# Cross attention scores and values, and the row sums of the prompt heads, as products of split parts

## The chip, the cores and the metric

The kernel runs on one core of a Trainium2 chip. The metric is device time in microseconds (us) of one execution; lower is better. The core has a matrix engine (TensorE, PE in the profile, with its weight loads listed as PEld), three engines for elementwise work (VectorE or DVE, ScalarE or ACT, GpSimd or POOL) and SyncE (SP), which issues most of the transfers. Each engine works through its own list of instructions in order, and semaphores tie the lists together.

## The reference, cut to what matters

One step of a decoder layer, for a prompt of 512 tokens and eight samples of four tokens that share all weights:

- h = RMSNorm(x); z = h W_in. Eight attention heads of 64 columns (three dilated patterns with a linear distance penalty) and four HGRN2 heads of 128. Each attention head's output is divided by its root mean square and multiplied by a gain.
- x = x + [attention ; HGRN2] W_out.
- Cross attention with four heads of 128 over a memory of 256 rows: cq = RMSNorm(x) W_cq; s = cq k^T / sqrt(128); p = softmax(s); x = x + (p v) W_co. For the prompt k and v are computed from `mem_prompt`; each sample has its own cached k and v.
- x = x + W_down( silu(conv3(RMSNorm(x) W_gate)) * (RMSNorm(x) W_up) ), then a last RMSNorm.

Everything is float32. The core of the cross attention is

```
cq = (c @ w_cq).reshape(B, T, X_H, X_DH)
s = jnp.einsum('bthd,bmhd->bhtm', cq, mem_k.astype(cq.dtype)).astype(f32) * (X_DH ** -0.5)
pr = jax.nn.softmax(s, axis=-1)
co = jnp.einsum('bhtm,bmhd->bthd', pr.astype(x.dtype), mem_v.astype(x.dtype)).reshape(B, T, X_W)
x = x + co @ w_co
```

and each attention head's norm is `a32 * rsqrt(mean(a32 * a32, -1) + EPS)` over its 64 columns.

## The kernel before, in words

**Layout.** Activations are held transposed: features on the 128 partitions, the 544 tokens (512 of the prompt, 32 of the samples) along the free dimension. Token columns are taken in two cuts, `CUTS` = 0 to 256 and 256 to 544.

**Split products.** The dense products do not use single precision operands. Each operand is split into a high part (a copy rounded to float32r, on ACT, or on DVE now and then) and a low part (the rest, a subtraction on DVE), and a product becomes three: high x high, high x low, low x high (`passes`, L922). Other products take their float32 operands directly, in one instruction of the program: scores, values, transposes' companions in the HGRN2 heads, sums over partitions.

**Stages.** First the input projections with the attention heads and the HGRN2 heads woven between them (tiles `ps_hv`, `ps_q`, `psS`, `psO` and so on), then memory keys and values (`ps_ck`, `ps_cv`), the output projection `ps_wo`, the cross attention (`ps_cq`, `ps_cp`, `ps_cpo`), its output projection `ps_co`, and the feed-forward part to the end.

**Order of the work.** The program is first recorded on a tape (`Tape`, L276) and then ordered: `due` (L417) gives each step a time by when it should begin, `order` (L462) goes through all engines with estimated durations, and `run` (L441) repeats this six times and keeps the best order. Dense products are marked main and keep the order in which they are written; all other PE work ("side" work: scores, transposes, values, row sums) is put between them when its inputs are estimated to be ready. So a change of any duration or of any operation can move every later step. Working tiles come from one pool of 71 buffers of 128 x 544 (`A`, L736, and `R`, L739, which gives a float32r tile of that pool); a step whose tile doesn't fit waits (`fits`, L544, `leaves_room`, L548). Scores, transposes and values write to a pool of five banks of PSUM (`PX`).

**The start** is kept in the order as written (L1036). SP loads the input blocks, the vectors, and the constants `cs`: identity, a matrix of ones, and `blk64`, ones in two diagonal blocks of 64, each 128 x 128. ACT squares each input block, DVE adds the squares, and `psr_mix` on PE sums them over partitions with the matrix of ones.

**Row sums.** `rsqrt_rows` (L964) multiplies squares with the ones or with `blk64`, so that every partition gets the sum, and ACT makes exp(-0.5 ln(.)) of it. `prompt_attention` (L1335) calls it for each of its four pairs of heads: `att` is the heads' output, `asq` its square, `psr_att` the sum, `ar` the factor.

**Cross attention.** `dense_by_half` (L942) computes the queries of all four heads for the first cut of the tokens, then of all four for the second; after each cut `cq_after` (L1911) runs for each head and calls `cross_prompt` (L1877), which handles 256 tokens: scores `ps_cp` (two products of 128 x 256), softmax into `cp`, four transposes `ps_cpt`, a copy `cpt`, values `ps_cpo` (two products of 128 x 256), and `split_psum` (L1809), which writes the high and low parts `coh` and `col` that the projection `ps_co` reads. The sample tokens have a path of their own: their queries go to `cqbd`, scores `ps_cs`, values `ps_cso`, gathered in `ps_cos`. `mk` and `mvt` are the prompt's memory keys and values.

Of the kernel before, what the change touches and what calls it, by code (L numbers as in the profile page):

```python
# [10 lines left out]
F32 = mybir.dt.float32  # L11
F32R = mybir.dt.float32r
AF = mybir.ActivationFunctionType
ALU = mybir.AluOpType
# [3 lines left out]
SEQ = 512  # L18
# [6 lines left out]
NMEM = 256  # L25
# [4 lines left out]
XH = 4  # L30
# [28 lines left out]
FW = N  # L59
# [663 lines left out]
def tile_decoder_step(ctx: ExitStack, tc: tile.TileContext, xT, memT, kwT, vw, s0, conv_in, mkT, mv, vecs, cst,  # L723
                      w_first, w_in, w_out, w_cq, w_ck, w_cv, w_co, w_gate, w_up, w_down,
                      yT, kT_out, vT_out, st_out, conv_out, mkT_out, mv_out, ss_out):
    nc = tape = Tape(tc.nc)

    one = ctx.enter_context(tc.tile_pool(name="one", bufs=1))
# [7 lines left out]
    def A(name, shape=None, dt=F32):  # L736
        return tape.tile(act, shape or [128, FW], dt, tag="a", name=name, bufs=NA)

    def R(name):  # L739
        return tape.tile(act, [128, FW], F32R, tag="a", name=name, bufs=NA)[:, :N]  # L740
# [24 lines left out]
    vec = tape.tile(one, [128, NVEC], F32, name="vec")  # L765
    nc.scalar.dma_start(vec[:, :KT], vecs[:, :KT])
    mid = CST_COLS["dbias"][0]
    cs = tape.tile(one, [128, mid], F32, name="cs")
    cs2 = tape.tile(strm, [128, NHELD - mid], F32, name="cs2")
    eps = tape.tile(one, [128, 1], F32, name="eps")  # L770
    nc.gpsimd.memset(eps, EPS)
# [3 lines left out]

    def C(name):
        lo, hi = CST_COLS[name]
        return cs[:, lo:hi] if hi <= mid else cs2[:, lo - mid:hi - mid]


    specs = []
# [171 lines left out]
    def split_into(hl, src, g, c0, c1):  # L953
        hi, lo = (t[:, c0:c1] for t in hl)
        nc.scalar.activation(hi, src, AF.Copy, scale=g)
        nc.vector.scalar_tensor_tensor(lo, src, g, hi.bitcast(F32), op0=ALU.mult, op1=ALU.subtract)

    def split_plain(src, name):
# [2 lines left out]
        nc.vector.tensor_tensor(lo, src, hi.bitcast(F32), op=ALU.subtract)  # L961
        return hi, lo

    def rsqrt_rows(acc, c0, c1, mat, width, r, name, rest=None):  # L964

        for n0, m in ((c0, c1 - c0),) if c1 - c0 <= 512 else CUTS:
            ps = (PX if rest is None else PDEC)(f"psr_{name}_{n0}")
            nc.tensor.matmul(ps[:, :m], mat, acc[:, n0:n0 + m], start=True, stop=rest is None)
            if rest is not None:
                nc.tensor.matmul(ps[:, :m], mat, rest[:, n0:n0 + m], start=False, stop=True)  # L970
            nc.scalar.activation(r[:, n0:n0 + m], ps[:, :m], AF.Ln, bias=eps, scale=1.0 / width)
            nc.scalar.activation(r[:, n0:n0 + m], r[:, n0:n0 + m], AF.Exp, scale=-0.5)

    class SumSq:
        def __init__(self, name, adder=nc.vector):
# [22 lines left out]
    def x_load(i, c0, c1):  # L998
        nc.sync.dma_start(xin[i][:, c0:c1], xT[128 * i:128 * i + 128, c0:c1])
# [4 lines left out]
    def warm_up(count, n=128):  # L1004

        for _ in range(count):
            nc.tensor.matmul(banks[0][1][:, :n], zero[:, :128], zero[:, :n], start=True, stop=True)
# [3 lines left out]
    def square(i):  # L1011
        if i:
            sqs.append(A(f"sq_mix{i}"))
        nc.scalar.activation(sqs[i][:, :N], xin[i][:, :N], AF.Square)

    def add_square(i):
        nc.vector.tensor_tensor(mix_acc[:, :N], mix_acc[:, :N], sqs[i][:, :N], op=ALU.add)
# [18 lines left out]
    with tape.as_written():  # L1036
        nc.scalar.preload_act_table_set(LN_SET)
        x_load(0, 0, 256)
        for c0, c1 in ((0, 128), (128, 384)):
            nc.sync.dma_start(wf[0][:, c0:c1], w_first[0][:, c0:c1])  # L1040
        x_load(0, 256, N)
        for i in range(1, KT):
            x_load(i, 0, N)
            nc.sync.dma_start(wf[i], w_first[i])
        nc.sync.dma_start(vec[:, KT:], vecs[:, KT:])
        nc.sync.dma_start(cs, cst[:, :mid])
        for i in range(3):
            ws.load(i)
        nc.sync.dma_start(cs2, cst[:, mid:NHELD])
        for _ in range(AHEAD - 1):  # L1050
            stream.load()
        zero = A("zero")
        nc.vector.memset(zero[:, :128], 0.0)
        with tape.main():
            warm_up(WARM)
        for i in range(KT):
            hi, lo = A(f"wfh{i}", [128, 384], F32R), A(f"wfl{i}", [128, 384], F32R)
            if i == 0:

                nc.vector.tensor_copy(hi[:, :128], wf[0][:, :128])  # L1060
                split_into(xs[0], xin[0][:, :256], V("norm_mix", 0), 0, 256)
                nc.scalar.copy(hi[:, 128:], wf[0][:, 128:])
                for c0, c1 in ((0, 128), (128, 384)):
                    nc.vector.tensor_tensor(lo[:, c0:c1], wf[0][:, c0:c1], hi[:, c0:c1].bitcast(F32), op=ALU.subtract)
                split_into(xs[0], xin[0][:, 256:N], V("norm_mix", 0), 256, N)
            else:
                split_into(xs[i], xin[i][:, :N], V("norm_mix", i), 0, N)
                nc.scalar.copy(hi, wf[i])
                nc.vector.tensor_tensor(lo, wf[i], hi.bitcast(F32), op=ALU.subtract)
            wf_hl.append((hi, lo))  # L1070
            if i > 1:
                square(i - 2)
            if i > 3:
                add_square(i - 3)
        square(KT - 2)
        add_square(KT - 3)
        square(KT - 1)
        add_square(KT - 2)
        add_square(KT - 1)

        for k in range(KT - 1):
            with tape.main():
                first_products(k)
        for n0, n in CUTS:
            ps = PD(f"psr_mix_{n0}")
            with tape.main():
                nc.tensor.matmul(ps[:, :n], C("ones"), mix_acc[:, n0:n0 + n], start=True, stop=True)
            nc.scalar.activation(r_mix[:, n0:n0 + n], ps[:, :n], AF.Ln, bias=eps, scale=1.0 / D)
            nc.scalar.activation(r_mix[:, n0:n0 + n], r_mix[:, n0:n0 + n], AF.Exp, scale=-0.5)
        with tape.main():  # L1090
            first_products(KT - 1)
# [243 lines left out]
    def prompt_attention(p, q, k, v):  # L1335
        pst = by_token(v, f"v{p}")
# [82 lines left out]
        po = PX(f"psO{p}")  # L1419
# [13 lines left out]
        att, sq, r = A(f"att{p}"), A(f"asq{p}"), A(f"ar{p}")  # L1433
        nc.scalar.copy(att[:, :SEQ], po)
        nc.scalar.activation(sq[:, :SEQ], po, AF.Square)
        rsqrt_rows(sq, 0, SEQ, C("blk64"), 64, r, f"att{p}")
        nc.vector.tensor_tensor(att[:, :SEQ], att[:, :SEQ], r[:, :SEQ], op=ALU.mult)
        att_parts(p)
        split_into(mixed[p], att[:, :SEQ], V("att_out_norm", p), 0, SEQ)
# [274 lines left out]
    ps = PX("psr_mem")  # L1714
# [7 lines left out]
    mk = [A(f"mk{i}", [128, 2, NMEM]) for i in range(2)]  # L1722
    mvt = [A(f"mvt{t}") for t in range(2)]
# [10 lines left out]
    for c in range(4):  # L1734
        ws.take()
        for i in range(2):
            hi, lo = (t.rearrange("p k c -> p (k c)") for t in ws.whole[ws.i - 1][i][:2])
            xh, xl = mems[2 * c + i]
            with tape.main():
                for t in range(2):  # L1740
                    tok = slice(128 * t, 128 * t + 128)
                    for j, (a, b) in enumerate(((xh, hi), (xl, hi), (xh, lo))):
                        nc.tensor.matmul(pcv[t], a[:, tok], b, start=(c == 0 and i == 0 and j == 0),
                                         stop=(c == 3 and i == 1 and j == 2))
# [60 lines left out]
    cqbd = tape.tile(strm, [128, NB, 4, 32], F32, tag="qbd", name="qbd_mem", bufs=1)  # L1805
    nc.gpsimd.memset(cqbd, 0.0)
    co_hl = [(R(f"coh{h}"), R(f"col{h}")) for h in range(XH)]

    def split_psum(h, ps, c0, c1):  # L1809
        hi, lo = (t[:, c0:c1] for t in co_hl[h])  # L1810
# [66 lines left out]
    def cross_prompt(h, part):  # L1877

        ps = PX(f"ps_cp{h}{part}")
        for a in range(2):  # L1880
            qb = 2 * part + a
            nc.tensor.matmul(ps[:, 256 * a:256 * a + 256], cqT[h][:, 128 * qb:128 * qb + 128],
                             mk[h // 2][:, h % 2, :], start=True, stop=True)
        if part:
            cross_sample_scores(h)
        pt = A(f"cp{h}{part}")
        den = softmax_exp(ps, pt, f"{h}{part}")
        softmax_scale(pt, den)
        pst = PX(f"ps_cpt{h}{part}")
        for c in range(2):  # L1890
            for a in range(2):
                nc.tensor.transpose(pst[:, 256 * c + 128 * a:256 * c + 128 * a + 128],
                                    pt[:, 256 * a + 128 * c:256 * a + 128 * c + 128], C("ident"))
        ptt = A(f"cpt{h}{part}")
        if part:
            nc.vector.tensor_copy(ptt[:, :512], pst)
        else:
            nc.scalar.copy(ptt[:, :512], pst)
        po = PX(f"ps_cpo{h}{part}")
        for c in range(2):  # L1900
            nc.tensor.matmul(po[:, :256], mvt[c][:, 128 * h:128 * h + 128], ptt[:, 256 * c:256 * c + 256],
                             start=c == 0, stop=c == 1)
        split_psum(h, po[:, :256], 256 * part, 256 * part + 256)

    cqT = [A(f"cq{h}") for h in range(XH)]

    def cq_evac(h, ps, n0, n):
        nc.vector.scalar_tensor_tensor(cqT[h][:, n0:n0 + n], ps[:, :n], 128.0 ** -0.5, r_cross[:, n0:n0 + n],
                                       op0=ALU.mult, op1=ALU.mult)

    def cq_after(h, c):  # L1911
        if c:
            nc.gpsimd.tensor_copy(cqbd[:, :, h, 4 * h:4 * h + 4],
                                  cqT[h][:, SEQ:N].rearrange("p (b t) -> p b t", t=TS))
        cross_prompt(h, c)
# [763 lines left out]
    for m in range(2 * LAST_PAIRS, KT):  # L2679
        held[m] = []  # L2680
        for c in range(0, k, 4):
            e = min(k - c, 4)
            t, hi, lo = (A(f"{n}z{m}_{c}", [128, e, 128], dt) for n, dt in (("wd", F32), ("wdh", F32R), ("wdl", F32R)))
# [21 lines left out]
    rest = [(m, c) for c in range(1, 2) for m in range(2 * LAST_PAIRS, KT)]  # L2705
    before.step(3)
    before.step(4)
    while rest:
        m, c = rest.pop(0)
# [81 lines left out]
```

## Time and profile before

| | |
|---|---|
| median of 3 runs | 807.85 us (807.83 to 808.33) |
| the profiled execution | 808.49 us, of which the span is 806.7 us |
| PE busy | 793.3 us, 98% of the span |
| DVE busy | 664.9 us, 82% |
| ACT busy | 466.8 us, 58% |
| POOL busy | 200.2 us, 25% |

The span is the time from the first to the last instruction that the profile records. Rows of the profile are read like this: "L718 PE MATMUL ps_cp<-mk,cq" is a matmul that writes tile ps_cp from mk and cq; L718 is the line of the recorder through which every operation passes, so tiles, not lines, tell operations apart. Matmuls overlap in the pipeline, so the mean of one record is longer than the time by which it moves the next; the rows of the chain, which give a start and a length for a whole run of matmuls, tell that.

### The profile page before, as it was taken

To read this page: it belongs to the slowest core of one execution; us is meant where nothing else is said; L and a number is where in the kernel's file an instruction comes from. 1 tells how busy PE (TensorE), PEld (TensorE's weight loads), DVE (VectorE), ACT (ScalarE), POOL (GpSimd) and SP (SyncE) were. 2 spreads that over 40 slices of the span, in tenths; PEclk is the share of its full clock that TensorE was granted. 3 is DMA by queue.
4 is the path that set the end of the run, shared out by engine and by line. 5 is a ranking of instruction groups with operands and counts; after the bars stand their busy time and mean duration, and the time that the engine had idled before them with its cause. 6 is when DMAs were issued, how large, how long until landed. Compare 5 with 4: busy or idle time off the path is not lost.

```text
span 806.7 us, 19149 instructions
## 1 busy us (share of the span) xinstructions
PE 793.3 (98%) x7432; PEld 745.7 (92%) x7432; DVE 664.9 (82%) x1484; ACT 466.8 (58%) x996; POOL 200.2 (25%) x282
## 2 busy tenths in 40 slices
PE   9999999999999999999999999999999999999995
PEld 8998878887888989999889999999999999999995
DVE  6899787488788885664579989998998998989973
ACT  7734468626458445544266657665665766668642
POOL 1131100031110200232134134442353352242023
PEclk9999999999999999999999999999999999999999
DMA  8744894998942355461654177778878878777203
GB/s 308 252 145 137 272 324 146 303 347 275 293 136 79 108 162 201 131 176 49 195 157 132 35 169 184 169 167 199 200 164 192 196 165 199 184 200 173 70 2 111
DMA packets 106699, 143.35 MB, mean 178 GB/s; under 512 B 7280, under 2 KB 73712, under 8 KB 106608
## 3 DMA queue, kind: packets, MB, share of 16 engines
q1 hardware_dynamic: 91296, 123.77, 48.4%
q0 software_dynamic: 14592, 17.83, 14.1%
q8 instruction: 58, 0.95, 0.5%
q10 hardware_dynamic: 720, 0.53, 0.2%
q14 instruction: 33, 0.27, 0.1%
HBM read 134.04 MB, written 8.07 MB: 176 GB/s over the span
## 4 chain that ended last, share of the span: by engine, by line
PE 89%; DVE 4%; ACT 3%; DMA 1%; issue 1%; SPq 0%; DVEq 0%; ACTq 0%
PE ps_au L718 7%; PE ps_ag L718 7%; PE ps_wo L718 6%; PE ps_aw L718 4%; PE ps_cu L718 4%; PE ps_cg L718 3%; PE ps_co L718 3%; PE ps_q L718 3%; PE ps_g L718 3%; PE ps_cq L718 3%; PE ps_dz L718 3%; PE ps_az L718 3%; PE ps_cw L718 2%; PE ps_hv L718 2%; PE ps_cv L718 2%; PE ps_du L718 2%
## 5 line engine op out<-in xcount | busy, mean ns | idle before, releaser
L718 DVE TENSOR_TENSOR wl<-wr,wh 128x512 fp32r<-128x512 f32 x102 | 74.2, 749 | 0.5 <-ACT wh L718 0.5
L718 ACT CAST wh<-wr 128x512 fp32r<-128x512 f32 x102 | 58.4, 618 | 12.3 <-DMA wr<-in_w_in 8.1
L718 POOL TENSOR_TENSOR hG<-hG,hf 128x256 f32<-128x256 f32 (+1 forms) x28 | 24.2, 864 | 135.8 <-DVE hf L718 69.7
L718 POOL COPY last<-ug 128x16 f32<-128x16 f32 (+1 forms) x44 | 32.5, 776 | 56.1 <-DVE ug L718 51.9
L718 DVE SCALAR_TENSOR_TENSOR cv<-ug,vec,cv 128x560 f32<-128x560 f32 x44 | 35.3, 801 | 2.1 <-ACT cv L718 1.5
L718 POOL TENSOR_TENSOR acc_cx<-acc_cx,sq_cx 128x256 f32<-128x256 f32 (+1 forms) x14 | 12.1, 864 | 63.1 <-PE ps_wo L718 36.6
L690 POOL DMA_DIRECT2D S13w<-in_w_down x12 | 12.6, 1048 | 48.2 <-DVE xr L718 13.9
L718 ACT ACTIVATE cv<-cv 128x560 f32<-128x560 f32 x22 | 14.8, 674 | 15.8 <-DVE cv L718 15.7
L718 ACT ACTIVATE cv<-ug,vec 128x560 f32<-128x560 f32 x22 | 18.9, 858 | 6.3 <-DVE ug L718 5.3
L718 PE MATMUL ps_co<-coh,wh 128*128 128x256 f32 (+1 forms) x64 | 19.3, 301 | 0.0
L718 ACT ACTIVATE P<-P,mx 128x128 f32<-128x128 f32 (+3 forms) x32 | 17.6, 555 | 2.5 <-DVE mx L718 2.5
L718 POOL COPY ug<-conv_state 128x16 f32<-128x16 f32 x22 | 18.5, 875 | 0.0
L718 PE MATMUL ps_co<-coh,wl 128*128 128x256 f32 (+1 forms) x64 | 18.4, 288 | 0.0
L718 PE MATMUL ps_co<-col,wh 128*128 128x256 f32 (+1 forms) x64 | 18.4, 288 | 0.0
L718 POOL TENSOR_TENSOR acc_final<-acc_final,sq_final 128x256 f32<-128x256 f32 (+1 forms) x10 | 8.6, 870 | 39.3 <-ACT sq_final L718 39.2
L718 DVE TENSOR_TENSOR xr<-xr,ps_wo 128x256 f32<-128x256 f32 (+1 forms) x16 | 6.9, 436 | 13.6 <-PE ps_wo L718 13.6
L718 ACT COPY keptg<-ps_ag 128x272 f32<-128x272 f32 x18 | 6.9, 386 | 18.4 <-PE ps_ag L718 18.4
L718 ACT ACTIVATE cp<-ps_cp,cmx 128x256 f32<-128x256 f32 x16 | 7.5, 472 | 15.2 <-DVE cmx L718 15.2
L718 POOL TENSOR_TENSOR acc_ux<-acc_ux,sq_ux 128x256 f32<-128x256 f32 (+1 forms) x13 | 11.6, 891 | 17.8 <-ACT sq_ux L718 17.6
L718 DVE TENSOR_TENSOR xr<-xr,ps_aw 128x272 f32<-128x272 f32 x36 | 15.6, 432 | 0.4 <-PE ps_aw L718 0.2
L718 PE MATMUL psd<-st,qbd_win 128*32 128x224 f32 x256 | 15.8, 358 | 0.0
L718 POOL TENSOR_SCALAR cp<-cp,cden 128x256 f32<-128x256 f32 x8 | 8.2, 1024 | 30.4 <-DVE cden L718 24.0
(3269 smaller groups left out, 3751.2 us busy)
## 6 DMA issues: line engine op xcount, KB each, us to landing
st<-in_kwT SPq DMA_DIRECT2D x32, 448.0 KB, 5.2
st<-in_vw SPq DMA_DIRECT2D x28, 512.0 KB, 6.0
wr<-in_w_in SPq DMA_DIRECT2D x25, 512.0 KB, 6.5
wru<-in_w_up SPq DMA_DIRECT2D x10, 512.0 KB, 4.9
wrg<-in_w_gate SPq DMA_DIRECT2D x9, 512.0 KB, 6.2
st<-in_mkT SPq DMA_DIRECT2D x8, 512.0 KB, 4.8
wr<-in_w_out SPq DMA_DIRECT2D x8, 512.0 KB, 4.3
S13w<-in_w_down SPq DMA_DIRECT2D x24, 128.0 KB, 3.6
```

The costliest lines, as they stand in the source:

```text
L690: return tape.put(engine, lambda: call(*args, **kw), outs, ins, 0.1, 0.3, size)
L718: return tape.put(engine, lambda: call(*args, **kw), outs, ins, length, lag, size, port, codes, work, mode)
```

## The change

The scores and the values of the prompt's cross attention and the row sums of the prompt's attention heads are computed from split operands. Three products take the place of one for scores and values, two for a row sum (its constant matrix needs no low part). The operands are split where they are made: memory keys and values once, queries after each cut, the probabilities when they are copied from PSUM, the squares in a new function `exact`. The constants' tile is cut in two: `cs` keeps the identity, and a new float32r tile `sums` holds the ones and `blk64`, loaded into a working tile `given` and copied by ACT. Products that still use the ones or `blk64` in single precision read the same tile as float32.

```diff
-    cs = tape.tile(one, [128, mid], F32, name="cs")
+    cs = tape.tile(one, [128, 128], F32, name="cs")
+    sums = tape.tile(one, [128, mid - 128], F32R, name="sums")
...
-        return cs[:, lo:hi] if hi <= mid else cs2[:, lo - mid:hi - mid]
+        if hi <= 128:
+            return cs[:, lo:hi]
+        return sums[:, lo - 128:hi - 128].bitcast(F32) if hi <= mid else cs2[:, lo - mid:hi - mid]
...
+    def exact(src, name, c0, c1, of=None):
+
+        hi, lo = (A(f"{p}_{name}_{c0}", [128, FW], F32R) for p in ("rh", "rl"))
+        nc.scalar.activation(hi[:, c0:c1], src[:, c0:c1] if of is None else of, AF.Copy if of is None else AF.Square)
+        nc.vector.tensor_tensor(lo[:, c0:c1], src[:, c0:c1], hi[:, c0:c1].bitcast(F32), op=ALU.subtract)
+        return hi, lo
+
     def rsqrt_rows(acc, c0, c1, mat, width, r, name, rest=None):
 
         for n0, m in ((c0, c1 - c0),) if c1 - c0 <= 512 else CUTS:
             ps = (PX if rest is None else PDEC)(f"psr_{name}_{n0}")
-            nc.tensor.matmul(ps[:, :m], mat, acc[:, n0:n0 + m], start=True, stop=rest is None)
+            parts = acc if isinstance(acc, tuple) else (acc,)
+            for i, part in enumerate(parts):
+                nc.tensor.matmul(ps[:, :m], mat if len(parts) == 1 else mat_r(mat), part[:, n0:n0 + m], start=i == 0,
+                                 stop=rest is None and i == len(parts) - 1)
...
+    def mat_r(mat):
+        return sums[:, 128 * mat:128 * mat + 128]
...
-        nc.sync.dma_start(cs, cst[:, :mid])
+        nc.sync.dma_start(cs, cst[:, :128])
+        given = A("given", [128, mid - 128])
+        nc.sync.dma_start(given, cst[:, 128:mid])
...
         square(KT - 2)
+        nc.scalar.copy(sums, given)
         add_square(KT - 3)
         square(KT - 1)
...
-        rsqrt_rows(sq, 0, SEQ, C("blk64"), 64, r, f"att{p}")
+        rsqrt_rows(exact(sq, f"att{p}", 0, SEQ), 0, SEQ, 1, 64, r, f"att{p}")
...
+    mv_hl = []
+    for t in range(2):
+        hi, lo = R(f"mvh{t}"), R(f"mvl{t}")
+        nc.scalar.copy(hi[:, :512], mvt[t][:, :512])
+        nc.vector.tensor_tensor(lo[:, :512], mvt[t][:, :512], hi[:, :512].bitcast(F32), op=ALU.subtract)
+        mv_hl.append((hi, lo))
...
-            nc.tensor.matmul(ps[:, 256 * a:256 * a + 256], cqT[h][:, 128 * qb:128 * qb + 128],
-                             mk[h // 2][:, h % 2, :], start=True, stop=True)
+            (hi, lo), (kh, kl) = (t[:, 128 * qb:128 * qb + 128] for t in cq_hl[h]), mk_hl[h]
+            for i, (l, r) in enumerate(((hi, kh), (hi, kl), (lo, kh))):
+                nc.tensor.matmul(ps[:, 256 * a:256 * a + 256], l, r, start=i == 0, stop=i == 2)
...
-        ptt = A(f"cpt{h}{part}")
-        if part:
-            nc.vector.tensor_copy(ptt[:, :512], pst)
-        else:
-            nc.scalar.copy(ptt[:, :512], pst)
+        ph, pl = R(f"cpth{h}{part}"), R(f"cptl{h}{part}")
+        nc.scalar.copy(ph[:, :512], pst)
+        nc.vector.tensor_tensor(pl[:, :512], pst, ph[:, :512].bitcast(F32), op=ALU.subtract)
         po = PX(f"ps_cpo{h}{part}")
         for c in range(2):
-            nc.tensor.matmul(po[:, :256], mvt[c][:, 128 * h:128 * h + 128], ptt[:, 256 * c:256 * c + 256],
-                             start=c == 0, stop=c == 1)
+            vh, vl = (t[:, 128 * h:128 * h + 128] for t in mv_hl[c])
+            for i, (l, r) in enumerate(((vh, ph), (vh, pl), (vl, ph))):
+                nc.tensor.matmul(po[:, :256], l, r[:, 256 * c:256 * c + 256], start=c == i == 0, stop=c == 1 and i == 2)
...
+    cq_hl = [(R(f"cqh{h}"), R(f"cql{h}")) for h in range(XH)]
+    mk_hl = []
+    for i in range(2):
+        hi, lo = (A(f"mk{p}{i}", [128, 2, NMEM], F32R) for p in "hl")
+        nc.scalar.copy(hi, mk[i])
+        nc.vector.tensor_tensor(lo, mk[i], hi.bitcast(F32), op=ALU.subtract)
+        mk_hl += [(hi[:, a, :], lo[:, a, :]) for a in range(2)]
...
     def cq_after(h, c):
+        hi, lo = (t[:, 256 * c:256 * c + 256] for t in cq_hl[h])
+        nc.scalar.copy(hi, cqT[h][:, 256 * c:256 * c + 256])
+        nc.vector.tensor_tensor(lo, cqT[h][:, 256 * c:256 * c + 256], hi.bitcast(F32), op=ALU.subtract)
```

## The prediction

> **What bounds the kernel now.** I read the page first: the busy shares, the clock and the chain that ended last.
>
> ```profile
> span 806.7 us, 19149 instructions
> ...
> PE 793.3 (98%) x7432; PEld 745.7 (92%) x7432; DVE 664.9 (82%) x1484; ACT 466.8 (58%) x996; POOL 200.2 (25%) x282
> ...
> PEclk9999999999999999999999999999999999999999
> ...
> PE 89%; DVE 4%; ACT 3%; DMA 1%; issue 1%; SPq 0%; DVEq 0%; ACTq 0%
> ```
>
> PE is busy 98% at full clock, and 89% of the chain lies on it. A busy share is a mean, so I looked next at the stretches that the change touches, and at PE's waits.
>
> ```profile
> core 0: us, PE busy (x) PEld busy (x) DVE busy (x) ACT busy (x) POOL busy (x), PEclk, DMA share, GB/s
> ...
> 359.30:375.00 15.70, 15.70 (x121) 15.17 (x121) 6.70 (x15) 6.06 (x17) 2.83 (x3) 1.00 0.35 106
> 375.00:404.00 29.00, 29.00 (x227) 24.65 (x227) 14.27 (x33) 10.74 (x34) 5.96 (x9) 1.00 0.51 153
> 404.00:437.00 33.00, 32.97 (x291) 30.50 (x290) 28.32 (x58) 23.20 (x62) 13.53 (x15) 1.00 0.49 150
> ```
>
> ```profile
> PE ps_au L718 <- ACT keptu L718: 1.1, 1, 1.1
> ```
>
> The cross attention runs from 359 to 437 us with no hole on PE. VectorE (DVE) and ScalarE (ACT) have slack up to 404; from 404 to 437 DVE is down to 33.00 - 28.32 = 4.7 us of it. PE's longest wait is 1.1 us, in another stage. So microseconds taken off PE here should come off the end, as long as nothing makes PE wait. The prices of the products stand in the chain:
>
> ```profile
> 136.53 1.06 PE psr_att L718 x2
> ...
> 286.56 0.86 PE psr_att L718 x2
> ...
> 305.64 5.56 PE ps_cv L718 x24
> ...
> 359.28 2.85 PE ps_cq L718 x24
> ...
> 365.88 0.86 PE ps_cp L718 x4
> ...
> 378.64 0.86 PE ps_cpo L718 x4
> ...
> 381.24 1.00 PE ps_cs L718 x16
> 382.24 1.06 PE ps_cpo L718 x4
> ```
>
> The reader is to see that a single precision product is two records: ps_cp x4 is two products of 256 columns in 0.86 us, 0.43 us each. A split product (float32r) is one record: 2.85 / 24 = 0.1188 us at 256 columns (ps_cq) and 5.56 / 24 = 0.2317 us at 512 (ps_cv). The group behind the narrow tiles of ps_cs takes 1.06 instead of 0.86: 0.20 us for the change of tile shape.
>
> **The change, part by part.** *Scores and values.* There are 8 groups of ps_cp and 8 of ps_cpo, two products each. Two products become six records: 6 x 0.1188 = 0.71 us instead of 0.86, a saving of 0.147 us a group and 16 x 0.147 = 2.36 us in all, on PE.
>
> *Row sums of the attention heads.* Four products of 512 columns at 0.86 us become two records each, 2 x 0.2317 = 0.46 us: 0.397 us saved, four times, 1.59 us. The block matrix holds only zeros and ones, so it needs no second part.
>
> PE saves 2.36 + 1.59 = 3.95 us.
>
> The Trainium skill ("TensorE: Matmul & The Clock Gate", section "Back-to-back issue gap") puts one warm matmul in a row at N / 2.4 + 2.5 ns, 109 ns at 256 columns and 216 ns at 512. By that the saving would be 16 x (0.86 - 0.655) + 4 x (0.86 - 0.43) = 5.0 us, an estimate from that page. The rows here are 9% and 7% longer than the page's figures, so the trace decides against it.
>
> *Work added on DVE and ACT.* The splits need copies and subtractions. Their prices:
>
> ```profile
> L718 DVE TENSOR_TENSOR wl<-wr,wh 128x512 fp32r<-128x512 f32 x102 | 74.2, 749 | 0.5 <-ACT wh L718 0.5
> L718 ACT CAST wh<-wr 128x512 fp32r<-128x512 f32 x102 | 58.4, 618 | 12.3 <-DMA wr<-in_w_in 8.1
> ```
>
> ```profile
> 4.45 0.41 ACT L718 CAST wfh<-wf 128x256 fp32r<-128x256 f32 x1 [0.82 <-DMA wf<-in_w_first]
> ...
> 4.89 0.42 DVE L718 TENSOR_TENSOR wfl<-wf,wfh 128x256 fp32r<-128x256 f32 x1 [0.54 <-ACT wfh L718]
> ```
>
> ```profile
> L718 ACT COPY cpt<-ps_cpt x4: 587/597/614, 374.6 to 383.8; 128x512 f32<-128x512 f32 x4
> L718 DVE COPY cpt<-ps_cpt x4: 679/688/692, 389.2 to 408.7; 128x512 f32<-128x512 f32 x4
> ```
>
> DVE: memory keys and values 4 x 0.75 = 3.0; eight query halves 8 x 0.42 = 3.4; probabilities, eight subtractions at about 0.69 where four copies stood, 4 x 0.69 = 2.8; row sums 4 x 0.75 = 3.0; together 12.2 us. ACT: 4 x 0.62 = 2.5, 8 x 0.41 = 3.3, 4 x 0.60 = 2.4, 4 x 0.62 = 2.5 and one copy of constants 0.4; together 11.1 us. What belongs to the cross attention, 9.2 us on DVE and 8.2 on ACT, finds 44.7 - 20.97 = 23.7 us of idle DVE and 44.7 - 16.8 = 27.9 us of idle ACT between 359.3 and 404. I cost it at nothing: the query products of the next heads (ps_cq, in program order) keep PE busy meanwhile. Without that cover it costs what the second rival below says.
>
> *Longer chains.* Each head's scores now wait for one copy and one subtraction of the query (0.41 + 0.42), its values for a subtraction more (0.69): about 1.5 us with nothing else in front. What waits for them is the output projection, ps_co. Its second half takes the last head and the sample tokens:
>
> ```profile
> 411.87 0.41 DVE L718 TENSOR_TENSOR col<-ps_cpo,coh 128x256 fp32r<-128x256 f32 x1
> ...
> 420.96 0.48 DVE L718 TENSOR_TENSOR col<-ps_cos,coh 128x32 fp32r<-128x32 f32 x4
> ```
>
> ```profile
> 423.46 3.41 PE ps_co L718 x24
> ```
>
> The prompt part is ready at 412.3, 11 us before the products at 423.46 that use it. The sample part is ready at 421.4, 2.0 us before. The sample chain reads the unsplit query and gains no operation; at worst its scores stand on PE behind the last head's, 0.83 us later, inside those 2.0 us. Cost zero; beyond the slack it would be one for one. In the attention stage the row sums' copy and subtraction (0.62 + 0.75) delay the normalised head; the last one counts:
>
> ```profile
> 300.88 0.75 DVE L718 SCALAR_TENSOR_TENSOR am3l<-att,vec,am3h 128x512 fp32r<-128x512 f32 x1
> ```
>
> ```profile
> 311.20 48.08 PE ps_wo L718 x384
> ```
>
> It is ready at 301.6, its first reader comes no earlier than 311.2: 9.6 us of cover for 1.4.
>
> *The constants at the start.* One load of 192 KB becomes two (64 and 128 KB), and ACT copies the second into the new tile, between the last two squares. What queues behind that copy is the last square, for which DVE's last addition and then psr_mix on PE wait.
>
> ```profile
> 11.64 0.33 SPq L690 DMA_DIRECT2D cs<-in_cst  x1
> 12.39 0.84 SPq L690 DMA_DIRECT2D wr<-in_w_in  x2
> ```
>
> ```profile
> cs<-in_cst SPq DMA_DIRECT2D x1, 192.0 KB, 5.1
> ```
>
> ```profile
> 17.59 1.76 ACT L718 ACTIVATE sq_mix<-x 128x544 f32<-128x544 f32 x3
> ...
> 19.07 3.21 DVE L718 TENSOR_TENSOR acc_mix<-acc_mix,sq_mix 128x544 f32<-128x544 f32 x4
> ```
>
> ```profile
> 22.34 1.18 PE L718 MATMUL psr_mix<-acc_mix,cs 128*128 128x256 f32 x4 [0.53 <-DVE acc_mix L718]
> ```
>
> The second load is issued one step later, at about 12.4, and lands at about 12.4 + 5.1 = 17.5; ACT reaches the copy after two of the three squares, at about 18.7. No wait, then. The last square ends at 19.35 + 0.41 = 19.8, while the last of the four additions starts at about 19.07 + 3 x 0.80 = 21.5 (3.21 / 4 = 0.80 each). It stays hidden with 1.7 us to spare, and the loads behind it on SP's queue move by one issue, 0.75 us (12.39 - 11.64). Cost zero; if the copy did wait for its load beyond that margin, the start would move one for one.
>
> *The plan.* The order of every engine is drawn up anew from the changed costs, and 71 buffers are shared. No row prices that. Below, I take the 1.1 us wait gone and four groups rid of their 0.20: -1.9 us. Above, one more wait of 1.1 us and ten more changes of shape at 0.20: +3.1 us. I take zero, since the dense products keep their order and PE's only wait in the middle of the run is small.
>
> **Sum.** The profiled execution took 808.49 us (span 806.7 and 1.8 outside it), 0.64 above the median of the runs, 807.85. 808.49 - 3.95 = 804.5; from the median, 803.9 us. With the bounds of the plan: 802.0 to 807.0.
>
> **The rivals.** *A plan that draws better.* The saving as above, with the wait before ps_au and four shape changes gone: 803.9 - 1.9 = 802.0 us. For it: the shorter products change every later time. Against it: only 1.1 us of waiting is there to win.
>
> *No change.* The plan draws worse by the upper bound, 803.9 + 3.1 = 807.0 us, 0.1% below before. For it: the narrow tiles of the decode heads are woven between these products, and where they fall is open. Also here: the split products do not run at 0.1188 beside narrow work but at 0.43 / 3 = 0.143 us, so that the change doesn't do what it says; ps_cq next to ps_cp in the chain speaks against that.
>
> *Slower: DVE becomes the bound of the output projection.* By the code, the second query half holds of the 71 buffers: 8 residuals, 16 parts of the normalised input, up to 16 of the query weights, 1 row factor, 4 memory tiles, 4 queries, 8 parts of the heads' outputs, 57 in all. The change adds 4 (memory parts) and 8 (query parts), 69 before any head's probabilities, which now take 3 a head. So the weight splits of the projection, done early before, can be pushed back, and head work with them. Before, five of them came ahead of 404, the first and the last:
>
> ```profile
> 372.77 0.93 DVE L718 TENSOR_TENSOR wl<-wr,wh 128x512 fp32r<-128x512 f32 x1
> ...
> 398.12 0.68 DVE L718 TENSOR_TENSOR wl<-wr,wh 128x512 fp32r<-128x512 f32 x1
> ```
>
> ```profile
> 372.59 1.01 POOL L718 TENSOR_SCALAR cp<-cp,cden 128x256 f32<-128x256 f32 x1 [2.68 <-DVE cden L718]
> ```
>
> If those 5 x 0.69 = 3.4 us and the 9.2 us of new DVE work all fall between 404 and 437, DVE has 28.3 + 12.6 = 40.9 us of work for 33: PE waits 7.9 us, 811.8 us. It decides from 4.7 us of moved work on; slower than before by more than 0.2% takes about 10. Against it: the query weights free four buffers with each head, and DVE is idle over half of the time before. The first of the two DVE rows is 0.25 us longer than the last: it ran beside the GpSimd scaling of the third row. The Trainium skill ("SBUF — State Buffer", section "Who interferes with whom") says that a VectorE operation with two SBUF inputs and a GpSimd operation that reads SBUF shut each other out for a whole instruction; by it the 16 new subtractions of that kind could each lose up to a GpSimd operation, which makes this rival dearer and leaves the forecast as it is. The row shows a part of such a block, not a whole one.
>
> **How the numbers follow.** The forecast, 803.9 with its own range 802.5 to 805.9: 58%. The better plan: 10%. No change: 20% (18 for the plan, 2 for the price of the products). Slower: 12%. A measurement of this kernel can tell about 0.2% (1.6 us) from no change, so faster is below 806.2 us: 58 + 10 = 68%; within: 20%; slower: 12%. The range for 8 in 10 reaches from 801.8 to 808.0: all of the forecast and the better plan and most of the third, not the slower case.
>
> **What would show it.** PE 7464 matmuls; ps_cp and ps_cpo 48 records each in groups of six over about 0.71 us, psr_att pairs over 0.46; the stretch from the first ps_cq to the last ps_co shorter by about 2.4 us, that up to the first ps_wo by 1.6. The start would be right if psr_mix begins at 22.3. The forecast is wrong if PE waits appear before ps_co, if DVE stands near 100% there while PE idles, if six records take 0.86, or if the stages after 437 give the saving back.

## The result, and the profile after

The changed kernel takes 802.6 us (802.35 to 802.98); before, in the same comparison, 807.84 (807.59 to 808.33). The ratio is 0.9935 with a 95% interval of 0.9918 to 0.9952: faster by 5.24 us, where 3.95 were forecast. The profiled execution has a span of 800.8 us.

The page of the changed kernel: span, busy times, granted clock by slices, and the share of each engine in the chain that ended last.

```profile
span 800.8 us, 19246 instructions
...
PE 789.3 (99%) x7464; PEld 746.9 (93%) x7464; DVE 671.3 (84%) x1504; ACT 475.9 (59%) x1017; POOL 191.7 (24%) x282
...
PEclk9999999999999999999999999999999999999998
...
PE 96%; DMA 1%; ACT 1%; DVE 0%; SPq 0%; issue 0%; DVEq 0%; ACTq 0%
```

PE has 32 records more and is busy 793.3 - 789.3 = 4.0 us less, at the same clock. PE's idle time, span less busy, went from 806.7 - 793.3 = 13.4 us to 800.8 - 789.3 = 11.5. So, by the matmul records, 4.0 us of the 5.9 between the two spans are work taken off PE and 1.9 are holes that closed; the records hide two more short waits, told with scores and values below. The execution profiled before was 0.64 us above the median, so 1.3 of these 1.9 are left between the medians.

The chain of the kernel before, rows that the prediction did not show (start, length, what):

```profile
25.78 5.97 PE ps_hv L718 x48
...
427.30 9.80 PE ps_co L718 x72
437.10 2.85 PE ps_g L718 x24
```

The same view of the changed kernel shows the products at their new prices, and where the stages begin.

```profile
25.12 6.01 PE ps_hv L718 x48
...
141.97 0.47 PE psr_att L718 x2
142.87 0.46 PE psr_att L718 x2
...
241.90 0.47 PE psr_att L718 x2
...
299.52 0.46 PE psr_att L718 x2
...
308.55 48.13 PE ps_wo L718 x384
356.68 2.84 PE ps_cq L718 x24
...
363.25 0.72 PE ps_cp L718 x6
...
379.69 1.86 PE ps_cs L718 x32
381.55 0.91 PE ps_cp L718 x6
382.45 0.44 PE ps_cpt L718 x4
382.89 0.72 PE ps_cpo L718 x6
...
384.04 3.17 PE ps_cq L718 x24
...
389.36 1.00 PE ps_cs L718 x16
390.36 3.37 PE ps_cq L718 x24
...
421.93 9.56 PE ps_co L718 x72
431.49 2.85 PE ps_g L718 x24
```

Six records take 0.70 to 0.72 us, two of 512 columns 0.46 to 0.47, and the 0.20 us behind the narrow ps_cs is paid by whichever group comes next: by ps_cp at 381.55, by ps_cq at 390.36 (3.37 against the 3.17 at 384.04, of the same cut of the tokens). From the first ps_hv to the first ps_wo it was 311.20 - 25.78 = 285.4 us and is 283.4; from the first ps_cq to ps_g it was 437.10 - 359.28 = 77.8 and is 74.8. The projection between them (48.1 both) and everything from ps_g to the end (369.6 and 369.3) did not move, so nothing was given back later.

PE's waits (what waited, for whom, us in total, times, longest), first of the kernel before, then of the changed one:

```profile
PE psr_mem L718 <- DVE acc_mem L718: 0.5, 1, 0.5
PE psr_mix L718 <- DVE acc_mix L718: 0.5, 1, 0.5
...
PE psL L718 <- ACT hsm L718: 0.2, 1, 0.2
```

```profile
PE ps_first L718 <- DVE zero L718: 1.1, 1, 1.1
PE ps_au L718 <- ACT keptu L718: 0.9, 1, 0.9
PE psr_final L718 <- ACT sq_last L718: 0.5, 1, 0.5
PE ps_ak L718 <- ACT keptk L718: 0.5, 1, 0.5
```

The three short waits of the first fence are not in the second. Busy time of PE by stretches places the holes; again before, then after:

```profile
core 0: us, PE busy (x), PEclk, DMA share, GB/s
0.00:25.00 25.00, 22.94 (x162) 1.00 0.92 321
25.00:308.00 283.00, 281.80 (x3389) 1.00 0.67 213
```

```profile
core 0: us, PE busy (x), PEclk, DMA share, GB/s
0.00:25.00 25.00, 23.86 (x167) 1.00 0.94 322
25.00:308.00 283.00, 282.52 (x3396) 1.00 0.66 213
```

The start loses 0.9 us of holes and the stage of the heads 0.7 (1.20 to 0.48). In the cross attention PE's records show none to lose. The start's part is mostly that of the one execution, as the point on the constants below shows; the 0.7 is the plan's.

### The profile page after: what moved, and what is told of

Same layout as the page of the kernel before. It is cut to its first block, busy times and chain, and to the rows that moved or that the text cites. A ratio compares the mean times of both kernels' runs of the same rounds, so it can differ in the third digit from the quotient of the medians.

```text
span 800.8 us, 19246 instructions
## 1 busy us (share of the span) xinstructions
PE 789.3 (99%) x7464; PEld 746.9 (93%) x7464; DVE 671.3 (84%) x1504; ACT 475.9 (59%) x1017; POOL 191.7 (24%) x282
## 4 chain that ended last, share of the span: by engine, by line
PE 96%; DMA 1%; ACT 1%; DVE 0%; SPq 0%; issue 0%; DVEq 0%; ACTq 0%
PE ps_au L718 7%; PE ps_ag L718 6%; PE ps_wo L718 6%; PE ps_aw L718 5%; PE ps_cu L718 4%; PE ps_cg L718 3%; PE ps_q L718 3%; PE ps_co L718 3%; PE ps_cq L718 3%; PE ps_g L718 3%; PE ps_dz L718 3%; PE ps_az L718 3%; PE ps_hv L718 2%; PE ps_cw L718 2%; PE ps_first L718 2%; PE ps_ck L718 2%
## 5 line engine op out<-in xcount | busy, mean ns | idle before, releaser
L718 POOL COPY last<-ug 128x2 f32<-128x2 f32 (+1 forms) x44 | 23.9, 573 | 93.2 <-DVE ug L718 86.5
L690 POOL DMA_DIRECT2D S13w<-in_w_down x12 | 12.8, 1064 | 22.3 <-PE ps_au L718 7.9
L718 PE MATMUL psdo<-st,dpt 128*32 128x256 f32 x224 | 15.5, 384 | 0.0
L690 POOL DMA_DIRECT2D A22w_0l<-in_w_down x6 | 11.0, 1839 | 16.9 <-PE ps_ag L718 8.7
```

Source lines behind the costliest of these rows:

```text
L690: return tape.put(engine, lambda: call(*args, **kw), outs, ins, 0.1, 0.3, size)
L718: return tape.put(engine, lambda: call(*args, **kw), outs, ins, length, lag, size, port, codes, work, mode)
```

## The experiments

Two theories. The first is the prediction's: PE's own products set the time, the added elementwise work is hidden, and the redrawn plan accounts for what is left. The rival: the elementwise work or the waits it brings cost something, or the gain comes from the redrawn plan and not from the products at all. The diffs are against the changed kernel, but for those of the planner, which fit either kernel.

### One part at a time

e1_rows: the four row sums and the new constants alone; scores, values and their operands are as before.

```diff
...
-            (hi, lo), (kh, kl) = (t[:, 128 * qb:128 * qb + 128] for t in cq_hl[h]), mk_hl[h]
-            for i, (l, r) in enumerate(((hi, kh), (hi, kl), (lo, kh))):
-                nc.tensor.matmul(ps[:, 256 * a:256 * a + 256], l, r, start=i == 0, stop=i == 2)
+            nc.tensor.matmul(ps[:, 256 * a:256 * a + 256], cqT[h][:, 128 * qb:128 * qb + 128],
+                             mk[h // 2][:, h % 2, :], start=True, stop=True)
...
```

> The row sums of the prompt heads alone are split (with the constants' new tile and their added copies and subtractions); scores and values of the cross attention stay single precision products. If the rows' prices carry the gain and the rest of it is the draw of the plan: 4 x 0.397 = 1.6 us less than before, 806.2 us, with 1.3 us either way for the plan. If the products are worth the whole measured gain in any plan: 5.24 x 1.59 / 3.95 = 2.1 us less, 805.7. If the added copies and subtractions cost something that the prices left out: no gain, 807.8 or more.

Measured: 805.3 us (805.13 to 805.9) beside 808.01, ratio 0.9965 (0.9953 to 0.9978): 2.7 us.

e2_cross: scores and values alone, with constants and row sums as before.

```diff
...
-        rsqrt_rows(exact(sq, f"att{p}", 0, SEQ), 0, SEQ, 1, 64, r, f"att{p}")
+        rsqrt_rows(sq, 0, SEQ, C("blk64"), 64, r, f"att{p}")
```

> Scores and values of the cross attention alone are split; the row sums and the constants are as before. Prices and plan: 16 x 0.147 = 2.4 us less than before, 805.5 us, with 1.3 us either way for the plan. Products worth the whole gain in any plan: 5.24 x 2.36 / 3.95 = 3.1 us less, 804.7. A hidden cost of the added work: 807.8 or more.

Measured: 805.38 us (804.62 to 805.78), ratio 0.9963 (0.9949 to 0.9977): 2.6 us. Each part gives its share, and the two add up to 5.3, the whole. That scores and values give 0.3 more than the 2.36 of the rows and the row sums 1.1 more than 1.59 can't be put down to the parts, since each run has an order of its own: in e1 the stage from ps_hv to ps_wo is 2.3 us shorter than before, but that from ps_cq to ps_g is too, by 0.6, with its products unchanged; in e2 the second is 2.9 shorter and the first 0.4 longer.

e3_splits: all copies and subtractions stay, all products, values and row sums too, go back to single precision on one part of each operand, which computes less than the reference.

```diff
...
-            for i, (l, r) in enumerate(((hi, kh), (hi, kl), (lo, kh))):
-                nc.tensor.matmul(ps[:, 256 * a:256 * a + 256], l, r, start=i == 0, stop=i == 2)
+            nc.tensor.matmul(ps[:, 256 * a:256 * a + 256], (hi, lo)[a], (kh, kl)[a].bitcast(F32), start=True, stop=True)
...
```

> All copies and subtractions of the change stay, 12.2 us on VectorE and 11.1 on ScalarE, but the products are single precision ones again, on one part of each operand (the other part's product is left out, so it computes less than the reference). If the added work is hidden behind PE: 807.8 us, with 1.3 us either way for the plan. If it costs something on the path, as in the rival in which VectorE binds the output projection: over 809, up to 811.8 - 803.9 = 7.9 us more.

Measured: 808.01 us (807.41 to 808.57) beside 808.01, ratio 0.9998 (0.9989 to 1.0007). The 12 us on DVE and 11 on ACT cost nothing here, within 0.1% either way. The order is redrawn here too, and the plans below move a kernel by about 1 us, so a cost smaller than that could hide; the rival in which elementwise work takes a large part of the gain falls.

### Does PE alone set the cross attention?

e6_hi: the changed kernel with one product in place of three for scores and values; copies and subtractions stay, and it computes less than the reference.

```diff
-            for i, (l, r) in enumerate(((hi, kh), (hi, kl), (lo, kh))):
-                nc.tensor.matmul(ps[:, 256 * a:256 * a + 256], l, r, start=i == 0, stop=i == 2)
+            for i, (l, r) in enumerate(((hi, kh) if a else (lo, kl),)):
+                nc.tensor.matmul(ps[:, 256 * a:256 * a + 256], l, r, start=True, stop=True)
...
```

> The changed kernel with one product instead of three for scores and values (each half takes one pair of parts; the other products are left out, so it computes less than the reference); all copies and subtractions stay. PE loses 64 products of 256 columns, 64 x 0.119 = 7.6 us. If PE sets the time of the cross attention and the other engines have slack: 802.6 - 7.6 = 795.0 us. If VectorE or the longer chains stand right behind PE there: the time falls by half of that or less, 799 us or more.

Measured: 795.25 us (795.18 to 795.84), ratio 0.9845 (0.9831 to 0.9858), 7.35 us below the changed kernel; 64 records fewer at 0.1188 are 7.6. The stage from ps_cq to ps_g goes from 74.8 to 67.4. Even with 7 us less on PE, DVE and ACT don't take over.

### How much is the plan?

Six runs draw the order anew without touching what is computed. e4 is the kernel before with the planner told the durations of the split products, e5 the changed kernel with the planner told those of the single precision ones; e7 and e8 are the two kernels with one constant of its costs changed, e11 and e12 with another.

```diff
+                if method == "matmul" and at.startswith("ps_cp"):
+                    length, codes = 3 * (0.000456 * n + 0.001), 6
+                if at.startswith("psr_att") and not at.startswith("psr_attS"):
+                    length = 2 * (0.000456 * n + 0.001)
```

That is e4. In e5 the two lengths are `2 * 0.00086 * n / 3` and `0.00086 * n`. The constants, e7 and e8, then e11 and e12:

```diff
-    SWITCH, NEAR = 0.14, 3.0
+    SWITCH, NEAR = 0.18, 3.0
```

```diff
-    SWITCH, NEAR = 0.14, 3.0
+    SWITCH, NEAR = 0.14, 2.0
```

> The kernel before, whose planner is told the durations of the split products for its single precision ones (0.35 us at 256 columns, 0.47 for a row sum): the work is that of before, the order another. If part of the gain is the draw of the plan: anywhere from 806.5 to 809.1 us (1.3 either way). If the gain sits in the products alone: 807.8 us.

> The changed kernel, whose planner is told the durations of the single precision products for the changed ones (0.44 us for three of 256 columns, 0.88 for the two of a row sum), so that the work is the same and the order another. If 1.3 us of the gain is a lucky draw of the plan: about 803.9 us. If the products are worth 5.2 us in any plan: 802.6 us.

> The kernel before with another plan: the planner's price of a change of tile shape is 0.18 us instead of 0.14; nothing else is changed. If the order is worth something: it lies away from 807.8 us, by up to 3 us. If not: 807.8 us.

> The changed kernel with the same other plan (0.18 us for a change of tile shape). If the products are worth 3.95 us and the rest was the draw: about 803.9 us, and about 3.95 us below the kernel before with that plan. If they are worth 5.2 us in any plan: 5.2 us below it.

> The kernel before with a third plan: the planner's preference for work of the same tile shape is 2.0 us instead of 3.0; nothing else is changed. As for the second plan: up to 3 us away from 807.8 us if the order is worth something.

> The changed kernel with the same third plan. The pairs so far (before and after, the second plan, and the two kernels told the other's durations) lie 5.2, 4.5 and 4.4 us apart. If the products are worth their prices from the rows: 3.95 us below the kernel before with this plan. If they are worth about half a microsecond more, for the changes of tile shape and the waits that go with them: 4.4 to 5.2 us below.

Measured, with PE's busy and idle time from each page (profiled execution):

| plan | before: us, PE busy, idle | after: us, PE busy, idle | time | busy |
|---|---|---|---|---|
| own | 807.84, 793.3, 13.4 | 802.6, 789.3, 11.5 | -5.24 | -4.0 |
| durations swapped (e4, e5) | 807.4, 793.4, 12.1 | 802.99, 789.3, 11.9 | -4.4 | -4.1 |
| SWITCH 0.18 (e7, e8) | 808.46, 794.2, 12.8 | 803.96, 790.1, 12.4 | -4.5 | -4.1 |
| NEAR 2.0 (e11, e12) | 808.42, 793.5, 12.8 | 803.17, 789.4, 11.8 | -5.25 | -4.1 |

The ratios to before are 0.9999 (0.9991 to 1.0008) for e4, 1.0009 (1.0 to 1.0018) for e7, 1.0007 (0.9999 to 1.0016) for e11, and 0.9935 (0.9923 to 0.9948) for e5, 0.9951 (0.9938 to 0.9965) for e8, 0.9943 (0.993 to 0.9955) for e12. A plan moves either kernel by up to 1.4 us; no median before comes within 3 us of one after. So a better draw alone is not the cause. The -4.4 of the swapped durations is taken across two occasions; each against the kernel before of its own occasion, e4 is 0.3 and e5 5.0 us faster, 4.7 apart. In each pair PE's busy time falls by 4.0 to 4.1, and what comes on top, 0.3 to 1.2 us, is idle time of PE and depends on the plan. Three of the four plans before leave 1.1 to 1.3 us of holes on PE between 25 and 308 us, three of the four after 0.5; but e4 has 0.5 as well, and e6, whose row sums are those of the changed kernel, has 1.15. The split into busy and idle time has a limit: in e2 PE is busy 1.4 less (791.9) at 2.6 us of gain, in e6 9.0 less (780.3) than the changed kernel at 7.35, because a plan also decides how often the 0.20 us is paid and how much PE idles.

The length of the stages is a steadier measure. In the four pairs, in the order of the table, the stretch from the first ps_hv to the first ps_wo gets 1.99, 1.43, 1.58 and 1.86 us shorter, where the rows said 1.59; that from the first ps_cq to ps_g 3.01, 2.80, 2.95 and 2.94, where they said 2.36.

### The price of a narrow product, and one step more

e10_narrow: the changed kernel with each split score product cut in two of 128 columns.

```diff
-            for i, (l, r) in enumerate(((hi, kh), (hi, kl), (lo, kh))):
-                nc.tensor.matmul(ps[:, 256 * a:256 * a + 256], l, r, start=i == 0, stop=i == 2)
+            for b in (0, 128):
+                for i, (l, r) in enumerate(((hi, kh), (hi, kl), (lo, kh))):
+                    nc.tensor.matmul(ps[:, 256 * a + b:256 * a + b + 128], l, r[:, b:b + 128], start=i == 0, stop=i == 2)
```

> The changed kernel with each split score product cut into two of 128 columns: 96 products of 128 instead of 48 of 256. If a split product's time goes by its columns alone (0.1188 us for 256, 0.0594 for 128): 802.6 us. If there is a share for each product, as 0.1188 - 256 / 2.4 GHz = 0.012 us: 48 x 0.012 = 0.6 us more, 803.2. If a narrow product costs as much as one of 256 columns: 48 x 0.119 = 5.7 us more, 808.3.

Measured: 807.99 us (807.51 to 809.0), ratio 1.0003 (0.9994 to 1.0012), 5.4 above the changed kernel: the whole gain is gone. Its chain, and three records in a row of its timeline:

```profile
363.68 1.29 PE ps_cp L718 x12
...
378.34 2.63 PE ps_cp L718 x24
```

```profile
363.80 0.28 PE L718 MATMUL ps_cp<-mkh,cqh 128*128 128x128 f32 x1
363.92 0.27 PE L718 MATMUL ps_cp<-mkl,cqh 128*128 128x128 f32 x1
364.02 0.27 PE L718 MATMUL ps_cp<-mkh,cql 128*128 128x128 f32 x1
```

The same multiplications in twice the records take 1.29 us instead of 0.71: 1.29 / 12 = 0.1075 each, and their starts lie 0.10 to 0.12 apart. Eight groups make 8 x 0.58 = 4.6 us; the stage grew by 4.9 (74.8 to 79.7), most of the rest lies in the start, 0.5 longer in this execution.

e9_hg: the changed kernel with the row sums of the HGRN2 heads split as well.

```diff
-            rsqrt_rows(sq, n0, n0 + n, C("ones"), 128, r, f"hg{h}")
+            rsqrt_rows(exact(sq, f"hg{h}", n0, n0 + n), n0, n0 + n, 0, 128, r, f"hg{h}")
```

> The changed kernel with the row sums of the four HGRN2 heads split in the same way (eight sums of 256 or 288 columns, with their copies and subtractions). In the changed kernel the four groups take 0.92 + 1.11 + 0.92 + 1.01 = 3.96 us on PE; as two split products each they take 4 x 2 x (0.119 + 0.132) = 2.0 us. If PE sets the time in that stage and the added elementwise work is hidden: 1.9 us less, 800.7 us, with 1 us either way for the plan. If the stage's VectorE, at 90% from 200 us on, is the limit: no gain, 802.6 us or more.

Measured: 801.28 us (801.05 to 801.6) beside 807.79, ratio 0.9918 (0.9905 to 0.9932). It is the fastest kernel of the study among those that compute the reference, 1.3 us below the changed one, run against run on different occasions; the two intervals against before overlap, and a plan alone moved the changed kernel by as much (1.4). The chain of the changed kernel and of this one, one head:

```profile
74.39 0.92 PE psr_hg L718 x4
```

```profile
77.18 0.51 PE psr_hg L718 x4
```

All heads together go from 0.92 + 1.11 + 0.92 + 1.01 = 3.96 us to 0.51 + 0.70 + 0.51 + 0.59 = 2.31. That is 1.65 by these rows; the stage from ps_hv to ps_wo is 1.3 shorter (283.4 to 282.1), and so is the whole.

## Why the prediction was right, and where its size was off

**What bounds the kernel: right.** The chain is now 96% PE, and e6 shows that a microsecond taken off PE in the cross attention comes off the end almost whole (7.35 of 7.6).

**Scores and values: right.** 0.71 us for a group of six, as worked out. The 16 groups of before stand in the chain with 14.41 us, those of after with 11.58; of the 2.83 between them two times 0.20 are shape changes that other groups now pay, which leaves the 2.4 of the prediction. The whole stage is 3.0 shorter, 0.6 more than "what would show it" said. Against e1, which has the products of before, it is 77.2 - 74.8 = 2.4; most of the other 0.6 is a longer stage in the kernel before. In its chain the last three quarters of the second half of ps_co, at 427.30, take 9.80 for 72 records, in the changed kernel 9.56; and the first quarter 3.41, where a third of 9.56 is 3.19. That is 0.46, and two short waits of the weight loads account for it (kernel before):

```profile
422.90 0.41 DVE L718 TENSOR_TENSOR xr<-xr,ps_co 128x256 f32<-128x256 f32 x1
...
423.43 0.19 PEld L718 LDWEIGHTS ps_co<-coh,wh 128*128 128x128 f32 x1 [0.20 <-issue]
...
429.94 0.44 DVE L718 TENSOR_TENSOR xr<-xr,ps_co 128x288 f32<-128x288 f32 x1
...
430.44 0.19 PEld L718 LDWEIGHTS ps_co<-coh,wh 128*128 128x128 f32 x1 [0.18 <-DVE xr L718]
```

The load at 430.44 waited for DVE's addition to the residual, which ended at 430.38. The load at 423.43 started 0.12 us behind the end of another such addition; that it waited for it is inferred, since the profile names no releaser there. PE's list of waits has neither, because the record of the matmul before lasts until the load starts (423.16 + 0.27 = 423.43). So the prediction's "no hole on PE" from 359 to 437 us was read off records that hide short waits. The wait for xr stands among the weight loads' waits of the kernel before, e7 and e11, and in no other run; the stage of e4, which lacks it, is still 2.8 us longer than that of e5, and why stays open. From 404 us to the end of ps_co DVE is busy 28.32 / 33.00 = 86% before and 20.64 / 27.50 = 75% after; that this closed the waits is likely, not shown.

**Row sums: near the forecast, with a price misread.** I priced four products of before at 0.86 us. In the chain quoted there, the first is 1.06, and one that the prediction did not look up, behind narrow tiles too, takes 0.96 from its start at 235.72 to the next group's at 236.68 in the timeline:

```profile
235.72 1.12 PE L718 MATMUL psr_att<-asq,cs 128*128 128x512 f32 x2
236.68 1.05 PE L718 MATMUL psU<-hvt,hkt 128*128 128x128 f32 x8
```

Together 1.06 + 0.86 + 0.96 + 0.86 = 3.74, against 0.47 + 0.46 + 0.47 + 0.46 = 1.86 after: 1.9 us by their own rows and not 1.59. In the other plans the four take 3.7 to 3.8 without the split. But these 0.3 did not reach the end: from the first ps_hv to the first ps_wo PE's busy time fell from 284.2 to 283.0, 1.3 us, and in the four pairs the whole stage got shorter by 1.4 to 2.0 with its holes and by 1.0 to 1.4 without. What the row sums paid for changes of shape before, other groups seem to pay after.

**The plan: the term that was off.** "I take zero, since the dense products keep their order and PE's only wait in the middle of the run is small", and, against the better plan, "only 1.1 us of waiting is there to win". Holes of 0.5 (psr_mem), 0.5 (psr_mix) and 0.2 us (psL) stood in the same list of waits below the one of 1.1, and I did not add them up. The first and the last belong to the stage of the heads and closed, 0.7 us, while the wait before ps_au that I had named went only from 1.1 to 0.9. The two waits in ps_co closed as well, 0.46. The result lies 1.3 below the forecast and 0.6 above the 802.0 of the better plan, which I had given 10%. The pairs with the same planner settings say that 0.3 to 1.2 us on top of PE's 4.0 is the usual outcome, so zero was the low end of this term rather than its middle. The closed waits come to 1.2 of the 1.3; the rest is no more than the reading of single executions. That PE's busy time fell by 4.0, so near to the 3.95, is partly luck: the 4.0 hold the 0.46 of hidden waits, while the stage of the heads gave 0.3 less than the 1.59 and PE was busy 0.3 longer ahead of the first ps_hv (23.7 to 24.0). Why the plans of the changed kernel leave PE fewer holes is not settled: that shorter products let the planner close them is an argument, and eight plans, with e4 and e6 against it, are too few to tell it from chance.

**Work added on DVE and ACT at nothing: right**, by e3 and by the stretches of the changed kernel:

```profile
core 0: us, PE busy (x) PEld busy (x) DVE busy (x) ACT busy (x) POOL busy (x), PEclk, DMA share, GB/s
356.70:404.00 47.30, 47.30 (x417) 44.66 (x416) 31.68 (x72) 25.76 (x76) 12.35 (x15) 1.00 0.52 165
404.00:431.50 27.50, 27.50 (x254) 25.71 (x253) 20.64 (x45) 18.36 (x46) 9.65 (x13) 1.00 0.42 129
```

The new work fell where DVE was idle, and PE's records are without a hole. In the output projection DVE has 6.9 us of slack where there were 4.7: the weight splits were not pushed back. The slower rival did not occur.

**The constants at nothing: right.** The start of the changed kernel: the copy of the constants, the last square, DVE's additions, and the products that use them.

```profile
17.91 0.39 ACT L718 CAST sums<-given 128x256 fp32r<-128x256 f32 x1
18.21 0.66 ACT L718 ACTIVATE sq_mix<-x 128x544 f32<-128x544 f32 x1
18.29 3.21 DVE L718 TENSOR_TENSOR acc_mix<-acc_mix,sq_mix 128x544 f32<-128x544 f32 x4
```

```profile
21.94 0.92 PE psr_mix L718 x4
```

The square ends at 18.9, well before the last addition starts (18.29 + 3 x 0.80 = 20.7), and psr_mix begins at 21.94 where 22.3 was said. Over all profiled executions the first ps_hv comes at 25.1 to 25.8 us with the old layout of the constants and at 25.1 to 26.0 with the new one, so the 0.6 between the two pages is no effect of the change.

**The page weighed in the prediction.** The estimate of 5.0 us from the Trainium skill ("TensorE: Matmul & The Clock Gate", "Back-to-back issue gap") lies nearer to 5.24 than 3.95 does, but not for its reason: the groups take 0.71 and 0.46 us as the rows had it, not 0.655 and 0.43, and PE's work fell by 4.0.

## What to carry to other kernels

Where the matrix engine is full, a float32 product of 256 or 512 columns replaced by split ones of the same width was worth about the difference of their rows, and the copies and subtractions were free where the stage had idle time on the elementwise engines. Add up all short waits of the full engine before you call the redrawn order neutral, those of its weight loads too, for the matmul records hide them. Price each group by its own row, for its neighbour's shape is in it. Check the width first: cut to 128 columns, a group of split scores takes 1.29 us, more than the 0.86 of the single precision products that it replaces.

## What was not expected of the hardware

A split product of 128 columns takes 0.1075 us, one of 256 columns 0.1188, one of 512 columns 0.2317. From 512 to 256 the price almost halves, from 256 to 128 it loses a tenth: there is a floor near 0.107 us for one record with its own weights, and in e10 it cost all of the gain. The changed kernel shows that the floor holds for much narrower records too. These are single precision, with 16 columns each:

```profile
413.52 1.85 PE L718 MATMUL ps_cos<-cs,com 128*128 128x16 f32 x16
```

The chain gives them 1.69 us, 1.69 / 16 = 0.106 each, with an eighth of the columns.

The Trainium skill ("TensorE: Matmul & The Clock Gate", "LDWEIGHTS (loading the stationary operand)") gives a weight load P / 1.2 ns, 107 ns for 128 columns. The floor agrees. That 16 columns cost as much as 128 speaks for the load, which is 128 columns wide in both, but no run here changes the load alone, so it isn't shown to be the cause.
